# Transposes of x1 in every fourth product step, and the last rows of x1 loaded two at a time, in an encoder block on one core

## The chip, the cores and the metric

The kernel runs as one program on one core of a Trainium2 chip. The metric is the device time of that program in microseconds (us). Before the change three runs gave 2173.34, 2176.47 and 2177.3 us, so the median is 2176.47 us.

## What is computed

One layer works on 2048 tokens of 1024 channels in float32. A mixer (input projection, a pooling branch, a convolution branch, gates, output projection) gives x1, and an MLP follows. Only its end matters here:

```python
x = x + rmsnorm(merged @ w_o[l], norm_mix_post[l])        # this sum is x1
h = rmsnorm(x, norm_mlp_pre[l])
f = jnp.square(jax.nn.relu(h @ w_up[l])) @ w_down[l]
x = x + rmsnorm(f, norm_mlp_post[l])
```

Here `w_up` is 1024 x 4096 and `w_down` is 4096 x 1024. The last line needs every row of x1 once more, after the last product.

## The kernel before, in words

**Numbers and halves.** Every operand of a product is held as a high part `hi` and a low part `lo`, and a product of two tiles is three matmul passes (hi-hi, hi-lo, lo-hi). The 2048 tokens are two halves `b` of 1024, and each half is two blocks `t` of 512. Products are done in Strassen's manner, with seven products `i` = 1 to 7 where eight plain ones would stand.

**The down stage.** The product with `w_down` is the last stage. It runs over four slabs `s` (rows of `w_down`), and `jobs` lists its steps: for slabs 0 to 2 the seven products of `DOWN`, each for both halves, and then slab 3 (`LAST`), first all seven products of `DOWN_LAST` = 1, 6, 7, 4, 2, 5, 3 for half 0 and then all seven for half 1. One product of slab 0 was already done earlier as filler, so 55 products stand in the list. `down_product` does a product as two steps `h` = 0, 1 of 24 matmuls each (`token_product`, matmuls on L1708), and adds each step's result to an accumulator in SBUF on VectorE (L120). So the stage has 110 product steps and 2640 matmuls.

**What a product needs.** `token_cells` loads a product's tokens (`tr<-fd`) into buffers of the pool TR (9 buffers of 128 x 1024), casts them to `hi` on ScalarE (L1688) and subtracts on VectorE to get `lo` (L123). `weights_down` loads the weights (`wr<-w_down`, in slab 3 also `wr<-wsum`), casts them on ScalarE (L1647 in slab 3) and gets their low part either on VectorE (`wl`, L123) or, in slab 3, by a load (`wl<-lows`). The low parts have three buffers (pool `pwl`), so the load of one waits until TensorE has finished with the weights three loads earlier. All these loads are issued by SyncE (`load`, L129), which takes its list in order: an entry that waits for a buffer holds up all that stand behind it.

**Background work.** After each product step `bg()` calls every `Lane`. A lane holds generators and a rate. At each call it takes up to `rate` pieces from its generator; a piece that yields a number n makes the lane skip the next n - 1 calls. Instructions of a lane are only ordered behind the main line's last instruction when the program's lists are made; on the chip they run when their engine's list comes to them.

**The transposes.** x1 lies in DRAM with channels on partitions (`x1d`). `turned` (L1770) makes a copy with tokens in rows (`x1t`) in 16 pieces: two loads of 256 KB into a TR buffer `x`, issued by GpSimd (`aside`, L133), `yield 2`, one transpose on VectorE into a second TR buffer `y` (L1784), four stores of 128 KB from `y`, again by GpSimd, and `yield`. Its lane has rate 2 and starts with the second product of the stage.

**The end.** For each half and block an object `Finish` waits until its accumulators are complete, takes squares on ScalarE (L1811) and multiplies by the gain on VectorE (`gain`, L126), computes the inverse root (`root`), loads rows of x1t in four pieces of 512 KB (`fetch`, `big<-x1t`, SyncE) into the pool BIG, adds the scaled result to them (`cell`, L1831) and stores them (`put`: GpSimd for half 0, SyncE for half 1). The blocks of half 0 do this in a lane during the products of half 1. The last block, (1, 1), uses `last_steps` for its loads and first gains; its end is `at_end`, called from inside the last product (`leave`, L1881, which also stores on SyncE). `last_steps` fetches all four pieces in the first call after it was made, that is, at the first product step of half 1.

Of the kernel before, what the change touches and what calls it, by code (L numbers as in the profile page):

```python
# [18 lines left out]
T = 512  # L19
G = T // P  # L20
# [47 lines left out]
def block_kernel(  # L68
# [15 lines left out]
    nc = tc.nc  # L84
# [17 lines left out]
    def nm(s):  # L102
        seq[0] += 1
        return f"{s}_{seq[0]}"

    def mk(pl, tag, dt=F32, shape=(P, TB)):
        return pl.tile(list(shape), dt, tag=tag, name=nm(tag))
# [4 lines left out]
    def two(ap):  # L112

        return ap.rearrange("p (c t) -> p c t", c=2)
# [4 lines left out]
    def add(o, a, b):  # L119
        return nc.vector.tensor_tensor(o, a, b, op=ALU.add)  # L120
# [4 lines left out]
    def mul(o, a, b):  # L125
        return nc.vector.tensor_tensor(o, a, b, op=ALU.mult)  # L126

    def load(o, src):
        return nc.sync.dma_start(o, src)  # L129

    def aside(o, src):

        return nc.gpsimd.dma_start(o, src)  # L133
# [8 lines left out]
    def mark(i):  # L142
        marks[i.ins.engine] = i.ins
        return i
# [119 lines left out]
    def psum(lab):  # L264
        return ps_mm.tile([P, TB], F32, tag="mm", name=nm(lab))
# [197 lines left out]
    def root_psum():  # L463
        return mk(ps_rb, "rb", F32, (P, T))
# [138 lines left out]
    def tr(dt=F32):  # L603
        return mk(*TR, dt)

    whole = tr()[:, :P]
# [927 lines left out]
    n = [0]  # L1534
# [29 lines left out]
    LAST = SLABS - 1  # L1564
    DOWN = (5, 6, 1, 3, 7, 4, 2)
    DOWN_LAST = (1, 6, 7, 4, 2, 5, 3)
    ENDS = {(0, 0): 2, (1, 0): 4, (1, 1): 5, (0, 1): 3}
    wsum, lows = {}, {}

    def last_weights():  # L1570
# [122 lines left out]
    chains, tiles = {}, {}  # L1693

    def banks(ps):
        return [ps[:, :T], ps[:, T:]]
# [41 lines left out]
    def recombine(b, pairs):  # L1738

        for to, of in pairs:  # L1740
            for o in (0, 1):
                add(acc[to, o, b], acc[to, o, b], acc[of, o, b])
                yield

    def last_product(i, h, b, w, cells):

        if i in (1, 2, 5):
            if i == 5 and b:
                chains[i, h] = [root_psum() if h else psum("down")[:, :T] for _ in (0, 1)]
            else:  # L1750
                tiles[i, h] = psum("down")
                chains[i, h] = banks(tiles[i, h])
        of = {1: 1, 6: 1, 7: 1, 4: 1, 2: 2, 5: 5, 3: 5}[i]
        ps, whole = chains[of, h], tiles.get((of, h))
        final = (i, b) == (DOWN_LAST[-1], 1)
        m, t = {1: (0, 0), 6: (0, 1), 7: (1, 1), 4: (1, 0), 2: (0, 0), 5: (1, 1), 3: (0, 1)}[i]
        c = acc[{(0, 0): 2, (0, 1): 3, (1, 0): 4, (1, 1): 5}[m, t], h, b]
        then = fin[b, t].at_end(h, c, ps) if final else None
        token_product(ps, w, cells, h, start=i in (1, 2, 5), stop=i in (4, 2, 3), after=then)
        if final:  # L1760
            return
        if i == 5 and b:
            for q, half in zip(ps, banks(c)):
                mark(add(half, half, q))
        else:
            mark(add(c, c, whole))
        if i == ENDS[m, t]:
            fin[b, t].ready[m, h] = c

    def turned():  # L1770
        for b in range(NB):
            for t in (0, 1):
                to = x1t[b, t].rearrange("(n tb i) (q k j) -> n q i tb k j", n=2, i=32, q=4, j=32)
                for c in (0, 2):
                    for n in (0, 1):
                        x, y = mk(*TR), mk(*TR)
                        s = slice(n * (T // 2), (n + 1) * (T // 2))
                        for k in (0, 1):
                            aside(
                                x[:, k * T : (k + 1) * T].rearrange("p (k n) -> p k n", k=2),  # L1780
                                two(x1d[b, c + k, t])[:, :, s],
                            )
                        yield 2
                        nc.vector.transpose(  # L1784
                            y.rearrange("p (tb k j) -> p k tb j", k=4, j=32),
                            x.rearrange("p (k tb j) -> p k tb j", k=4, j=32),
                        )
                        for q in range(4):
                            aside(
                                to[n, q][:, :, 2 * c : 2 * c + 4],  # L1790
                                y[32 * q : 32 * q + 32].rearrange("p (tb k j) -> p tb k j", k=4, j=32),
                            )
                        yield
# [4 lines left out]
    class Finish:  # L1798
# [36 lines left out]
            return [self.ready[m, g // 2][:, s] for m in (0, 1)]  # L1835

        def put(self, g):
            (load if self.b else aside)(out[self.b, self.t, g], self.x[g])

        def steps(self, lag):  # L1840
            for k in ((0, 0), (0, 1), (1, 0), (1, 1)) if self.t == 0 else ((1, 0), (1, 1), (0, 0), (0, 1)):
                while k not in self.ready:
                    yield 1
                self.gain(*k)
                yield
            for g in range(2):
                self.fetch(g)
            r = self.root(0, G)
            yield lag
            for g in range(G):  # L1850
                if g + 2 < G:
                    self.fetch(g + 2)
                self.cell(g, r[:, g : g + 1], self.parts(g))
                self.put(g)
                yield

        def last_steps(self):
            for g in range(G):
                self.fetch(g)
            for k in ((1, 0), (1, 1)):  # L1860
                while k not in self.ready:
                    yield 1
                self.gain(*k)
                yield

        def at_end(self, h, c, ps):
            y = tr()
            halves = [slice(i * T, (i + 1) * T) for i in (0, 1)]

            def arrive(gg):  # L1870
                s = halves[gg]
                mark(add(c[:, s], c[:, s], ps[gg]))
                self.squares(0, h, c[:, s], gg)
                mul(y[:, s], c[:, s], gains[0][:, :T])

            def leave(g, r):
                to = out[self.b, self.t, g]
                part = [y[:, halves[g % 2]], self.ready[1, h][:, halves[g % 2]]]
                x = self.x[g]
                for m, s in list(enumerate(halves))[::-1]:  # L1880
                    nc.vector.scalar_tensor_tensor(x[:, s], part[m], r, x[:, s], op0=ALU.mult, op1=ALU.add)  # L1881
                    load(to[:, s], x[:, s])

            def after(gg):
                with tc.high_priority(offset=URGENT):
                    arrive(gg)
                    if gg:
                        r = self.root(2 * h, 2 * h + 2)
                        for g in (0, 1):
                            leave(2 * h + g, r[:, g : g + 1])  # L1890

            return after

# [46 lines left out]
    for n, (s, i, b) in enumerate(jobs):  # L1940
        if s < LAST and i == DOWN[0] and b == 0:
            part = weights_down(s)
        if s == LAST and i == DOWN_LAST[0]:
            part = weights_down(s)
            if b == 0:
                gains.append(mk(p_ws, "ws"))
                load(gains[0], post)
                junk.append(mk(p_ws, "ws"))
                lanes += [Lane(3, fin[0, 0].steps(3), fin[0, 1].steps(3))]
            else:  # L1950
                lanes += [Lane(2, fin[1, 0].steps(1)), Lane(2, fin[1, 1].last_steps())]
        if s == LAST or b == 0 or (s, i) in [(0, i) for i in FIRST]:
            w = [part(i, o) for o in (0, 1)]
        if s == 0 and b and i in FIRST:
            for o in (0, 1):
                acc[i, o, 0] = mk(*BIG)
                load(acc[i, o, 0], fill[i, o])
        if n == 1:
            lanes.append(Lane(2, turned()))
        cells = coming.pop(0)  # L1960
        while len(coming) < (2 if s == LAST else 1) and n + 1 + len(coming) < len(jobs):
            job = jobs[n + 1 + len(coming)]
            coming.append(token_cells(*job, BIG if n < 4 else TR))
        down_product(s, i, b, w, cells)
        if s == LAST - 1 and i == 1:
            lanes.append(Lane(1, recombine(b, ((2, 1), (1, 6), (7, 1), (1, 5), (3, 1)))))
        if s == LAST - 1 and i == 7:
            lanes.append(Lane(1, recombine(b, ((4, 7), (5, 7)))))
        if (s, i, b) == (LAST - 1, DOWN[-1], 1):
            empty()  # L1970
# [71 lines left out]
```

## Time and profile before

| | |
|---|---|
| median of three runs | 2176.47 us |
| the profiled execution's own time | 2174.86 us |
| its span, first to last instruction | 2173.1 us |
| around the span | 1.76 us |
| TensorE matmuls busy | 2135.3 us, 98% |
| VectorE busy | 1716.1 us, 79% |
| ScalarE busy | 1034.3 us, 48% |
| mean DMA rate | 266 GB/s |
| mean granted clock of TensorE | 0.995 |

Times in the trace count from the span's start. The down stage fills the part from 1539 us on. In a row of the timeline stand the start, the length, the engine, the line, the operation with its tiles, a count, and in brackets the idle time ahead of it and what ended it. A row of waits has the total, the number of times and the longest. SPq is SyncE's list of DMA issues, and `DMA tr<-x1d` is the time from a DMA's issue to its landing. A matmul is shown with its whole passage (0.39 us), but one starts every 0.227 us when nothing holds it up.

### The profile page before, as it was taken

To read this page: it belongs to the slowest core of one execution; us is meant where nothing else is said; L and a number is where in the kernel's file an instruction comes from. 1 tells how busy PE (TensorE), PEld (TensorE's weight loads), DVE (VectorE), ACT (ScalarE), POOL (GpSimd) and SP (SyncE) were. 2 spreads that over 40 slices of the span, in tenths; PEclk is the share of its full clock that TensorE was granted. 3 is DMA by queue.
4 is the path that set the end of the run, shared out by engine and by line. 5 is a ranking of instruction groups with operands and counts; after the bars stand their busy time and mean duration, and the time that the engine had idled before them with its cause. 6 is when DMAs were issued, how large, how long until landed. Compare 5 with 4: busy or idle time off the path is not lost.

```text
span 2173.1 us, 25018 instructions
## 1 busy us (share of the span) xinstructions
PE 2135.3 (98%) x9424; PEld 1759.1 (81%) x9424; DVE 1716.1 (79%) x1664; ACT 1034.3 (48%) x1119; POOL 74.8 (3%) x131
## 2 busy tenths in 40 slices
PE   9999999999999999999999999999999999999996
PEld 7778888888888888888888888888887788888875
DVE  8999788999789999997777857876655775687557
ACT  6444453334534655445635766665443332223442
POOL 0000000000000000000000000000122300000000
PEclk9999999999999999999999999999999999999998
DMA  4789998688897787336686768986987775445896
GB/s 177 267 301 330 342 353 311 228 286 305 320 342 271 262 303 268 136 116 233 249 335 227 267 249 307 360 284 240 345 277 280 257 257 173 163 145 187 298 365 235
DMA packets 167498, 578.54 MB, mean 266 GB/s; under 512 B 20304, under 2 KB 24528, under 8 KB 167376
## 3 DMA queue, kind: packets, MB, share of 16 engines
q1 hardware_dynamic: 145616, 501.42, 64.4%
q10 hardware_dynamic: 12672, 46.14, 5.5%
q0 software_dynamic: 9088, 29.37, 3.9%
q8 instruction: 74, 1.21, 0.2%
q14 instruction: 48, 0.39, 0.1%
HBM read 381.20 MB, written 195.65 MB: 265 GB/s over the span
## 4 chain that ended last, share of the span: by engine, by line
PE 73%; DVE 9%; DMA 9%; issue 5%; ACT 2%; POOL 1%; SPq 0%; DVEq 0%; ACTq 0%; POOLq 0%
PE up L252 28%; PE down L1708 18%; PE wo L252 7%; PE glu L252 5%; PE B L252 4%; PE ga L252 3%; PE gb L252 3%; DVE y L910 3%; PE pool L252 2%; DMA tr<-x1d 2%; PE A L252 2%; DMA wl<-lows 1%; DMA tr<-fd 1%; POOL x1t L133 1%; DVE wl L123 1%
## 5 line engine op out<-in xcount | busy, mean ns | idle before, releaser
L252 PE MATMUL up<-big,wh 128*128 128x512 f32 x1792 | 480.9, 390 | 1.2 <-DVE big L123 0.8
L252 PEld LDWEIGHTS up<-big,wh 128*128 128x128 f32 x1792 | 335.8, 188 | 71.9 <-DVE big L123 1.1
L209 ACT CAST wh<-wr 128x1024 fp32r<-128x1024 f32 x167 | 175.5, 1052 | 314.9 <-PE up L252 68.5
L1708 PE MATMUL down<-wh,tr 128*128 128x512 f32 x784 | 307.0, 392 | 3.2 <-DVE tr L123 3.2
L910 DVE SCALAR_TENSOR_TENSOR y<-v,cst,y 128x1024 f32<-128x1024 f32 x240 | 307.0, 1279 | 2.4
L1708 PE MATMUL down<-wh,fo 128*128 128x512 f32 x776 | 298.6, 390 | 0.5 <-ACT wh L209 0.5
L252 PE MATMUL up<-big,wl 128*128 128x512 f32 x896 | 275.9, 389 | 0.0
L1708 PE MATMUL down<-wl,fo 128*128 128x512 f32 x760 | 235.1, 391 | 3.0 <-DVE wl L123 3.0
L209 ACT CAST wh<-ws 128x1024 fp32r<-128x1024 f32 x124 | 130.5, 1053 | 220.1 <-PE up L252 74.7
L252 PEld LDWEIGHTS up<-big,wl 128*128 128x128 f32 x896 | 168.2, 188 | 35.1
L1688 ACT CAST fo<-tr 128x1024 fp32r<-128x1024 f32 x86 | 90.4, 1051 | 219.2 <-DMA tr<-fd 90.8
L123 DVE TENSOR_TENSOR wl<-ws,wh 128x1024 fp32r<-128x1024 f32 x116 | 141.4, 1219 | 46.8 <-ACT wh L209 46.3
L1708 PEld LDWEIGHTS down<-wh,tr 128*128 128x128 f32 x784 | 148.0, 189 | 35.2 <-DVE tr L123 4.3
L1708 PEld LDWEIGHTS down<-wh,fo 128*128 128x128 f32 x776 | 145.9, 188 | 31.4 <-ACT wh L209 0.9
L1708 PEld LDWEIGHTS down<-wl,fo 128*128 128x128 f32 x760 | 142.7, 188 | 34.6 <-DVE wl L123 5.3
L123 DVE TENSOR_TENSOR wl<-wr,wh 128x1024 fp32r<-128x1024 f32 x111 | 135.1, 1218 | 26.0 <-ACT wh L209 22.9
L120 DVE TENSOR_TENSOR big<-big,down 128x1024 f32<-128x1024 f32 (+1 forms) x84 | 99.8, 1189 | 70.4 <-PE down L1708 70.3
L123 DVE TENSOR_TENSOR tr<-tr,fo 128x1024 fp32r<-128x1024 f32 x86 | 104.7, 1219 | 46.2 <-ACT fo L1688 46.0
L252 PE MATMUL glu<-big,wh 128*128 128x512 f32 x432 | 117.5, 393 | 3.0 <-ACT tr L408 2.5
L252 PE MATMUL wo<-big,wh 128*128 128x512 f32 x448 | 120.2, 390 | 0.0
L252 PE MATMUL gb<-big,wh 128*128 128x512 f32 x448 | 120.1, 390 | 0.0
L252 PE MATMUL ga<-big,wh 128*128 128x512 f32 x448 | 119.8, 389 | 0.0
(208 smaller groups left out, 3383.0 us busy)
## 6 DMA issues: line engine op xcount, KB each, us to landing
tr<-fd SPq DMA_DIRECT2D x110, 512.0 KB, 4.5
wr<-w_down SPq DMA_DIRECT2D x68, 512.0 KB, 6.3
wl<-kept SPq DMA_DIRECT2D x67, 512.0 KB, 5.2
kept<-wl SPq DMA_DIRECT2D x66, 512.0 KB, 5.7
wr<-w_up SPq DMA_DIRECT2D x64, 512.0 KB, 4.5
wr<-w_in SPq DMA_DIRECT2D x56, 512.0 KB, 6.0
fd<-tr ACTq DMA_DIRECT2D x54, 512.0 KB, 3.5
fd<-tr SPq DMA_DIRECT2D x48, 512.0 KB, 3.3
```

The lines of the kernel that those rows point to most:

```text
L120: return nc.vector.tensor_tensor(o, a, b, op=ALU.add)
L123: return nc.vector.tensor_tensor(o, a, b, op=ALU.subtract)
L133: return nc.gpsimd.dma_start(o, src)
L209: nc.scalar.copy(hi[:, :n], src[:, :n])
L252: i = nc.tensor.matmul(ps, w[wp][:, (at + k) * P : (at + k + 1) * P], rhs[k][xp], start=start and n == 0, stop=stop and n == len(order) - ...
L910: nc.vector.scalar_tensor_tensor(acc, v[:, k : k + TB], wk, acc, op0=ALU.mult, op1=ALU.add)
L1688: nc.scalar.copy(hi, t)
L1708: i = nc.tensor.matmul(ps[gg], cells[j][xp][:, c * T + at : c * T + at + P], w[j][wp][:, c * T : (c + 1) * T], start=start and first, stop ...
```

## The change

It does two things. In `turned` the number behind the loads goes from 2 to 4, so that a lane of rate 2 does a piece of the transposing in every fourth product step. In `last_steps` the four loads no longer stand ahead of everything: block (1, 1) first waits for its accumulator (1, 0), takes its gain, and then asks for rows 0 and, at the next piece, 1; then the same for (1, 1) and rows 2 and 3. Those two accumulators are complete after the two steps of product 5 of half 1, the last but one product.

The other lines of the diff give the same values, the same queue and the same order as before for every job in the list: `ENDS` comes out with the same numbers, the keys of `chains` and `tiles` get a third part, `put` names the queues that `load` and `aside` stand for, no `lag` is zero, and `after` takes the same roots and rows.

```diff
@@ last_product
-            if i == 5 and b:
-                chains[i, h] = [root_psum() if h else psum("down")[:, :T] for _ in (0, 1)]
+            tiles.pop((i, h, b), None)
+            if (i == 5 and b and h == 0) or (b and h and i == 5):
+                chains[i, h, b] = [root_psum() if h else psum("down")[:, :T] for _ in (0, 1)]
@@ turned
-                        yield 2
+                        yield 4
                         nc.vector.transpose(
@@ put
-            (load if self.b else aside)(out[self.b, self.t, g], self.x[g])
+            (nc.gpsimd if self.b == 0 else nc.sync).dma_start(
+                out[self.b, self.t, g], self.x[g]
+            )
@@ steps
-            yield lag
+            if lag:
+                yield lag
@@ last_steps
-            for g in range(G):
-                self.fetch(g)
-            for k in ((1, 0), (1, 1)):
+            for n, k in enumerate(((1, 0), (1, 1))):
                 while k not in self.ready:
                     yield 1
                 self.gain(*k)
                 yield
+                self.fetch(2 * n)
+                yield
+                self.fetch(2 * n + 1)
+                yield
```

More of the change, by code (lines that the diff above doesn't have):

```diff
@@ L1566, in block_kernel @@
     DOWN_LAST = (1, 6, 7, 4, 2, 5, 3)
-    ENDS = {(0, 0): 2, (1, 0): 4, (1, 1): 5, (0, 1): 3}
+    ENDS = {(0, 0): max((1, 2), key=DOWN_LAST.index), (1, 0): 4, (0, 1): 3, (1, 1): max((5, 7), key=DOWN_LAST.index)}
     wsum, lows = {}, {}
@@ L1747, in last_product @@
         if i in (1, 2, 5):
-            if i == 5 and b:
-                chains[i, h] = [root_psum() if h else psum("down")[:, :T] for _ in (0, 1)]
-            else:
-                tiles[i, h] = psum("down")
-                chains[i, h] = banks(tiles[i, h])
+            tiles.pop((i, h, b), None)
+            if (i == 5 and b and h == 0) or (b and h and i == 5):
+                chains[i, h, b] = [root_psum() if h else psum("down")[:, :T] for _ in (0, 1)]
+            else:
+                tiles[i, h, b] = psum("down")
+                chains[i, h, b] = banks(tiles[i, h, b])
         of = {1: 1, 6: 1, 7: 1, 4: 1, 2: 2, 5: 5, 3: 5}[i]
-        ps, whole = chains[of, h], tiles.get((of, h))
+        ps, whole = chains[of, h, b], tiles.get((of, h, b))
         final = (i, b) == (DOWN_LAST[-1], 1)
@@ L1761, in last_product @@
             return
-        if i == 5 and b:
+        if whole is None:
             for q, half in zip(ps, banks(c)):
@@ L1886, in after @@
                     arrive(gg)
-                    if gg:
-                        r = self.root(2 * h, 2 * h + 2)
+                    if h:
+                        if gg:
+                            r = self.root(2, 4)
+                            for g in (2, 3):
+                                leave(g, r[:, g - 2 : g - 1])
+                    elif gg:
+                        r = self.root(0, 2)
                         for g in (0, 1):
-                            leave(2 * h + g, r[:, g : g + 1])
+                            leave(g, r[:, g : g + 1])
             return after
@@ L1944, in block_kernel @@
             part = weights_down(s)
+        if s == LAST and i == DOWN_LAST[0]:
             if b == 0:
```

## The prediction

> **What bounds the kernel now.** I read the page first: the busy times of the engines.
>
> ```profile
> PE 2135.3 (98%) x9424; PEld 1759.1 (81%) x9424; DVE 1716.1 (79%) x1664; ACT 1034.3 (48%) x1119; POOL 74.8 (3%) x131
> ```
>
> TensorE is busy for 98% of the span, so a change that touches no matmul can only win what TensorE loses by standing still, or what it loses by a slower clock. Both parts of this change lie in the down stage, so I looked next at that stage in the chain of waits, and at TensorE's last matmuls in the timeline.
>
> ```profile
> 1539.37 27.21 PE down L1708 x120
> ...
> 1760.03 298.62 PE down L1708 x1316
> ...
> 2115.76 12.44 DMA wl<-lows
> ```
>
> ```profile
> 2159.61 0.61 PE L1708 MATMUL rb<-wl,big 128*128 128x512 f32 x2
> ```
>
> The first of these rows gives the pace: 27.21 / 120 = 0.2268 us from one matmul to the next. The code has 55 products of 48 matmuls in the stage, 2640 in all, which would take 2640 x 0.2268 = 598.7 us. The stage takes from 1539.4 to about 2160.2, 620.8 us. So it loses 22.1 us, and that is the most that both parts together can bring. From 1760.03 on there is one unbroken piece of 298.62 us for 1316 matmuls (0.2269 each): nothing is lost there. The losses lie ahead of 1760, while the transposes run, and behind 2058, in the last slab. The view of who waited for whom, for TensorE, names them:
>
> ```profile
> PE down L1708 <- DMA wl<-lows: 8.0, 3, 6.2
> PE down L1708 <- DVE tr L123: 3.2, 2, 1.8
> PE down L1708 <- DVE wl L123: 3.0, 4, 1.3
> PE down L1708 <- ACT wh L209: 0.5, 1, 0.5
> ```
>
> Asked by stretches, the same view puts the last three rows between 1640 and 1760, and the first, the loads of low parts, behind 2058. They add up to 14.7 us of pure waiting; the other 7.4 us of the 22.1 are matmuls at a slower pace after a wait.
>
> **First part: the transposes.** Work is only moved: 16 transposes, 32 loads and 64 stores stay. First the row of the change itself, VectorE's timeline around one transpose, and TensorE's at the same time:
>
> ```profile
> 1651.27 1.25 DVE L1784 STREAM_TRANSPOSE tr<-tr 128x1024 f32<-128x1024 f32 x1 [3.32 <-DMA tr<-x1d]
> 1652.44 1.18 DVE L123 TENSOR_TENSOR tr<-tr,fo 128x1024 fp32r<-128x1024 f32 x1
> ```
>
> ```profile
> 1653.68 0.50 PE L1708 MATMUL down<-wh,tr 128*128 128x512 f32 x1 [1.80 <-DVE tr L123]
> ```
>
> VectorE stood for 3.32 us in front of the transpose because its piece of x1d had not landed. The next entry of VectorE's list makes the low part of a token tile, and TensorE waited 1.80 us for exactly that. The chain of waits shows why the load is late:
>
> ```profile
> 1660.43 3.12 DMA tr<-x1d
> ...
> 1663.62 1.26 DVE tr L1784
> ```
>
> From one transpose (1651.27) to the next (1663.62) a closed loop runs: transpose, four stores issued by GpSimd, two loads issued behind them, landing, transpose. It took 12.35 us. The lane asks for a transpose every second product step, that is every 48 x 0.2268 = 10.9 us. The loop is longer than its period, so VectorE waits in front of transposes again and again. The view of the tensor x1d gives the total, with the number of times:
>
> ```profile
>   DVE tr L1784: 29.6, 8
> ```
>
> With a transpose in every fourth step the period is 21.8 us, 9.4 us more than the loop. The 29.6 us of VectorE's waiting should vanish nearly whole. The second thing that late pieces do is to keep TR buffers. SyncE's own waits, from 1540 to 1760 and then from 1760 to 1910, are led by:
>
> ```profile
> SPq L129 <- DMA x1t<-tr: 60.4, 14, 8.5
> ```
>
> ```profile
> SPq L129 <- PE down L1708: 97.6, 28, 7.8
> ```
>
> While transposes run, SyncE's loads of tokens wait for buffers that the stores of x1t have not given back; without them SyncE only waits for TensorE, which is the healthy case. At half the rate each buffer `y` still waits for its stores, but there is twice as long between two of them. The buffer `x` on the other hand is now taken for 64 product steps, about 350 us, where it was taken for 32.
>
> The price: of the 22.1 us, the last slab has 9.1 (below) and about 2 around the two small waits for low parts (8.0 - 6.2 = 1.8 us, with a little slow pace). The rest, 22.1 - 9.1 - 2 = 11 us, belongs to the transposes. Bounds: all 11 us are won, or none, if the shortage of buffers and not the wait for x1d carries it, or a loss, if the shortage lasts twice as long (a rival below). I take 8 us, near the upper end, because the quoted wait of TensorE follows directly on a wait for x1d, and leave 3 for waits by buffers. What is added at 1760 to 1900 is 16 / 2 = 8 transposes of 1.25 us on VectorE, hidden by the unbroken TensorE piece in that stretch; if that cover is gone they cost at most 10 us.
>
> **Second part: the last rows.** TensorE's timeline around the longest wait:
>
> ```profile
> 2121.69 0.39 PE L1708 MATMUL down<-wh,tr 128*128 128x512 f32 x1
> 2128.25 1.22 PE L1708 MATMUL down<-wl,big 128*128 128x512 f32 x2 [6.17 <-DMA wl<-lows]
> ...
> 2135.57 0.40 PE L1708 MATMUL down<-wh,fo 128*128 128x512 f32 x1
> ```
>
> By the code 20 matmuls lie between the first start of this fence plus one pace (2121.92) and the last row. At pace they take 4.54 us and would end at 2126.46; they end at 2135.57. So the wait of 6.2 us costs 9.1 us, 2.9 of them because the first matmuls behind it run at about half speed (1.22 us where a pair has 0.61). [...] The trace has the duration, so 9.1 is used.
>
> The load that came late was issued at 2115.76 and took 12.44 us. What SyncE issued ahead of it:
>
> ```profile
> 2097.32 1.37 SPq L129 DMA_DIRECT2D big<-x1t  x3
> ...
> 2107.71 0.43 SPq L129 DMA_DIRECT2D big<-x1t  x1
> 2108.24 0.87 SPq L129 DMA_DIRECT2D wr<-wsum  x2
> 2109.16 1.40 SPq L129 DMA_DIRECT2D big<-x1t  x2
> 2110.66 1.19 SPq L129 DMA_DIRECT2D wr<-wsum  x2
> 2113.07 1.54 SPq L129 DMA_DIRECT2D big<-x1t  x2
> ```
>
> Eight pieces of x1t go out in 16 us. Four belong to block (0, 1), which is due then; by the order of the lanes the first four are those of `last_steps`, not needed before 2162. What the DMA engines can move shows in the row of the stretch from 2050 to 2100:
>
> ```profile
> 2050.00:2100.00 50.00, 48.15 (x212) 39.22 (x211) 33.40 (x46) 25.06 (x43) 2.14 (x4) 1.00 0.94 350
> ```
>
> They are full (0.94) at 350 GB/s, so a piece of 512 KB takes 1.5 us, and four pieces 6.0 us. Without them the late load lands at about 2128.2 - 6.0 = 2122.2. TensorE wants it at 2121.92. So the wait of 6.2 us shrinks to some 0.3 us, too short for the clock, and 8.6 us of the 9.1 are won. Bounds: none, if the load is late for its other neighbours; 9.1, if it is on time. I take 8.
>
> What is late next: VectorE's additions, which give PSUM tiles back.
>
> ```profile
> 2119.12 2.74 DVE L1831 SCALAR_TENSOR_TENSOR big<-big,sy,big 128x512 f32<-128x512 f32 x4 [7.83 <-DMA big<-x1t]
> ...
> 2127.83 1.21 DVE L120 TENSOR_TENSOR big<-big,down 128x1024 f32<-128x1024 f32 x1
> ```
>
> Block (0, 1) waits 7.83 us for its own rows of x1t, and the addition behind it ends at 2129.0. Product 5 begins half a product behind 2135.57, at 2138.3; with the wait for low parts gone it would ask for that tile 9.1 us sooner, near 2129.2. This just fits, and as these rows too now have four pieces less ahead of them, it should fit easily.
>
> The moved loads: rows 0 and 1 go out during product 5, rows 2 and 3 during product 3. SyncE has these entries there now, and VectorE wants the rows at:
>
> ```profile
> 2151.52 18.34 SPq L129 DMA_DIRECT2D out<-big  x12
> ```
>
> ```profile
> 2162.54 2.74 DVE big L1881 x4
> ...
> 2166.76 0.75 DVE big L1881
> ```
>
> ```profile
> DMA to landing us min/median/max: 4.4/9.3/12.4
> ```
>
> Rows 2 and 3 are asked for behind the first step of product 3 (2138.3 + 10.9 + 5.4 = 2154.6), ahead of most of the stores, and land at the median (9.3) at 2163.9, 2.9 us before their use. I charge nothing for them. Work and bytes are the same in both kernels.
>
> **The sum.** 8 and 8 us are 16 us. On the profiled execution's own time this is 2174.9 - 16 = 2158.9; that execution is 1.6 us under the median of the runs, so the time to expect is 2160.5, rounded to 2160. The other edits give the same values and cost nothing.
>
> **The rivals.** (a) Only one part works. Either the shortage of TR buffers carries the loss ahead of 1760 and stays, or the low parts stay late for 2 to 6 us because of block (0, 1)'s rows, or the loads of `last_steps` are put early in SyncE's list all the same, since they are only ordered behind the main line. Each leaves one gain of about 8: 2168. For it speaks the 60.4 us of SyncE's waiting; against it that the two stalls are in different places with different causes.
>
> (b) The rows come late. [...] As a mechanism here: the list of SyncE puts rows 2 and 3 behind the stores of rows 0 and 1, which wait for the first four L1881 (end 2165.3). Then they land 4.4 to 12.4 us later, at 2169.7 to 2177.7, where 2166.76 is wanted: 3 to 11 us at the end that nothing hides, 2163 to 2171. Against it: VectorE's work ahead of that is long, so the loads should be ready first when the list is made.
>
> (c) Slower: `x` holds one of nine TR buffers for twice as long, and SyncE's shortage lasts for twice as many products. If the 60.4 us of waiting become 120.8 and TensorE pays the same share as now (11 / 60.4 = 18%), the first part loses 11 us more and the second wins 8: 2179. It is slower than before by over 0.2% from a share of (11 + 8 + 4.4) / 120.8 = 19% on; at 25%, 30 us, it gives 2176.5 + 19 - 8 = 2187. For it: after 1760 there is no slack in TR that the trace would show. Against it: these waits are 14 for 16 transposes, so they seem to go with the transposes, whose number stays, and not with the products.
>
> **The numbers.** My forecast has 0.58, (a) 0.16, (b) 0.09, (c) 0.17. A difference of 0.2%, 4.4 us, is about what a measurement of this kernel can tell from none. Faster by more: all of the forecast, 0.13 of (a), 0.07 of (b), together 0.78. Within it: 0.03 of (a), 0.02 of (b), 0.08 of (c), together 0.13. Slower: 0.09, from (c). The range goes from 2152, where the 22.1 us are won whole on the profiled execution, to 2174, past (a) and (b); outside are most of (c) and a little beneath.
>
> **What would show it.** Right: in the new profile VectorE waits for x1d no more than a few us in total, transposes run to about 1900, no TensorE wait of over 1 us lies ahead of 1900, the low part of product 2 in half 1 lands within 7 us, and four loads of x1t stand behind 2130. Wrong: SyncE's waits for x1t's stores grow beyond 60 us with TensorE waits for `tr` or `wl` behind 1760; or L1881 waits for x1t at the end; or the wait for `lows` in the last slab stays at some us.

## The result, and the profile after

The changed kernel took 2157.2 us (median of four runs, 2155.84 to 2159.0) and the kernel before 2176.76 us (four runs, 2173.34 to 2177.3). The ratio is 0.9914 with a 95% interval of 0.9897 to 0.9931: faster by 0.86%, or 19.6 us by the medians, where 16 were forecast. The two profiled executions differ by 2174.86 - 2156.01 = 18.85 us. One execution of the changed kernel in a later call, the profiled one there, was granted a mean clock of 0.39 and took 5387 us, and one of the kernel before 0.774 and 2599 us; no median, ratio or trace below counts them.

The head of the page after, and the long pieces of the down stage in its chain of waits (start, length, what):

```profile
PE 2128.9 (99%) x9424; PEld 1756.7 (82%) x9424; DVE 1716.3 (80%) x1664; ACT 1034.6 (48%) x1119; POOL 74.8 (3%) x131
```

```profile
1539.61 530.99 PE down L1708 x2340
2070.62 6.64 DMA wl<-lows
2077.31 7.56 PE down L1708 x32
2086.78 9.52 DMA big<-x1t
...
2100.14 23.43 PE down L1708 x101
```

```profile
2140.62 0.61 PE L1708 MATMUL rb<-wl,big 128*128 128x512 f32 x2
```

Where there was a patchwork of transposes, GpSimd issues and loads between 1570 and 1760, one piece of 2340 matmuls now stands, at 530.99 / 2340 = 0.2269 us each. The stage takes from 1539.5 to 2141.2, 601.8 us. By the working of the prediction it lost 22 us before; now it loses 601.8 - 598.7 = 3 us. What TensorE waits for in the stage:

```profile
PE down L1708 <- DVE tr L123: 1.5, 1, 1.5
...
PE down L1708 <- DMA wl<-lows: 0.4, 1, 0.4
```

Both waits lie in the last slab. The transposes, in the view of x1d (the issues of its loads with first and last start, and who waited for them):

```profile
L133 POOL DMA_DIRECT2D tr<-x1d x32: 713/723/736, 1535.9 to 1873.6; - x32
...
  DVE tr L1785: 2.9, 1
```

The last of these loads goes out at 1874 where it went out at 1736, the last transpose starts at 1905 where it started at 1748, and VectorE waits once for 2.9 us, not eight times for 29.6. SyncE's own waits from 1540 to 1760 are led by others than x1t's stores:

```profile
SPq L129 <- DVE wl L123: 62.2, 7, 16.0
SPq L129 <- DVE ws L123: 46.9, 6, 15.1
```

SyncE's list ahead of the load that had come late, and at the end:

```profile
2096.14 0.42 SPq L129 DMA_DIRECT2D big<-x1t  x1
2096.65 0.86 SPq L129 DMA_DIRECT2D wr<-wsum  x2
2097.56 0.93 SPq L129 DMA_DIRECT2D big<-x1t  x2
2105.71 14.12 SPq L129 DMA_DIRECT2D wl<-lows  x4
...
2139.22 0.38 SPq L129 DMA_DIRECT2D big<-x1t  x1
2141.59 0.34 SPq L1839 DMA_DIRECT2D out<-big  x1
2141.98 0.43 SPq L129 DMA_DIRECT2D big<-x1t  x1
```

```profile
2147.77 0.75 DVE big L1887
```

The load of low parts that had come late is now issued at 2105.71. In the 18.5 us ahead of it three pieces of x1t go out where eight did, and the last two pieces are issued at 2139.2 and 2142.0, between stores of block (1, 0). VectorE takes row 2 at 2147.77 with no wait. It starts on row 3 at 2149.2.

### The profile page after: what moved, and what is told of

It reads as the page before. It is cut to its first block, busy times and chain, and to the rows that moved or that the text cites. A ratio compares the mean times of both kernels' runs of the same rounds, so it can differ in the third digit from the quotient of the medians.

```text
span 2154.2 us, 25028 instructions
## 1 busy us (share of the span) xinstructions
PE 2128.9 (99%) x9424; PEld 1756.7 (82%) x9424; DVE 1716.3 (80%) x1664; ACT 1034.6 (48%) x1119; POOL 74.8 (3%) x131
## 4 chain that ended last, share of the span: by engine, by line
PE 85%; DVE 8%; DMA 3%; issue 2%; ACT 1%; SPq 0%; DVEq 0%; ACTq 0%
PE up L252 28%; PE down L1708 26%; PE wo L252 7%; PE glu L252 5%; PE B L252 4%; PE gb L252 4%; PE A L252 4%; PE ga L252 4%; PE pool L252 3%; DVE y L910 3%; DMA kept<-ws 1%; DVE tr L120 1%; DVE wl L123 1%; PE rb L458 1%; DVE ws L123 0%
## 5 line engine op out<-in xcount | busy, mean ns | idle before, releaser
L120 DVE TENSOR_TENSOR big<-big,down 128x1024 f32<-128x1024 f32 (+1 forms) x84 | 100.2, 1193 | 74.1 <-PE down L1708 74.0
```

## The experiments

Eleven kernels ran beside the changed one, each the changed kernel with one edit. The table has the median, the ratio to the kernel before on the same chip with its interval, and from the profiled execution what the down stage lost: its length less 598.7 us, and, summed from the gaps between matmuls and rounded, what of it lies in its first 400 us and behind. The split is good to about 1 us. The kernels were timed in several calls and on more than one chip, so the ratio compares better than the median.

| kernel | median us | ratio | lost | first 400 us | behind |
|---|---|---|---|---|---|
| before | 2176.8 | 1 | 22 | 10 | 12 |
| changed | 2157.2 | 0.9914 [0.9897, 0.9931] | 3 | 0 | 3 |
| yield 4 alone | 2161.7 | 0.9935 [0.9910, 0.9959] | 9 | 0 | 9 |
| late rows alone | 2173.0 | 0.9982 [0.9968, 0.9996] | 19 | 14 | 5 |
| yield 3 | 2171.7 | 0.9974 [0.9961, 0.9987] | 17 | 14 | 3 |
| yield 2, loads first | 2161.9 | 0.9932 [0.9906, 0.9958] | 9 | 5 | 4 |
| rows 0, 1 early | 2161.6 | 0.9932 [0.9906, 0.9958] | 6 | 0 | 6 |
| yield 1 | 2222.0 | 1.0207 [1.0179, 1.0235] | 65 | 60 | 5 |
| one TR buffer less | 2159.9 | 0.9917 [0.9899, 0.9935] | 4 | 0 | 4 |
| yield 2 from product 20 | 2165.2 | 0.9945 [0.9928, 0.9963] | 12 | 1 | 11 |
| yield 3 from product 2 | 2171.7 | 0.9991 [0.9977, 1.0005] | 19 | 16 | 3 |
| yield 4 from product 2 | 2160.3 | 0.9936 [0.9918, 0.9953] | 6 | 1 | 5 |
| yield 5 | 2170.9 | 0.9982 [0.9968, 0.9995] | 16 | 11 | 5 |

The changed kernel was also timed a second time, beside the last three kernels of the table:

> The changed kernel itself once more, beside these three on the same chip, to see how far one execution differs from another: 2157 us within 2, TensorE loses 3 to 5 us in the down stage.

Its median was 2158.5 us, the ratio 0.9935 [0.9911, 0.9959] where the first timing gave 0.9914. The executions of one kernel in one call lie up to 13 us apart (the kernel before: 2170.72 to 2183.37), so a few us between two medians of four executions are nothing to explain. What was expected of its stage has no trace to check it.

The other edits of the diff have no run of their own, but the traces of the first two runs below bear on them. With yield 2 every engine works through the same order of operations and tiles as in the kernel before up to 2097 us, and with the old `last_steps` the same order from 1978 us on, where those edits lie. So there are two parts to try.

**Each part alone.** `last_steps` as before with yield 4, and yield 2 with the new `last_steps`:

```diff
# yield 4 alone: last_steps as before        # late rows alone
-            for n, k in enumerate(...):     -                        yield 4
+            for g in range(G):              +                        yield 2
+                self.fetch(g)
+            for k in ((1, 0), (1, 1)):
...
-                self.fetch(2 * n)
...
-                self.fetch(2 * n + 1)
...
```

> The first part alone: yield 4, the last rows asked for early as before. My theory (the two losses are separate, each part removes its own): 11 us less than the kernel before, about 2166 us; no TensorE wait ahead of 1900 us; the wait for lows in product 2 of half 1 stays, 5 to 7 us. Rival (the gain comes from one part, and the other rode along): either 2157 us, or 2176 us.

> The second part alone: yield 2, the last rows late. My theory: 8 us less than the kernel before, about 2168 us; the waits for tr and wl between 1640 and 1760 us stay at some 6 us, the wait for lows falls under 1 us. Rival (the gain comes from one part): 2157 or 2176 us.

Measured: 2161.7 and 2173.0 us. The traces bear out that each part removes its own loss: the pace 10 to 14 us in the first 400 us, the rows 6 us behind (9 to 3 with yield 4, 12 to 5 with yield 2). In the times the pace alone is worth 14 us by the medians and 9 to 20 by the interval, where 11 were expected. The rows alone are worth 3 us by the medians and 1 to 7 by the interval, where 8 were expected. And yield 4 alone has the ratio of the changed kernel's second timing, 0.9935. So what the rows add to the pace is read from single traces; the times do not resolve it. TensorE's waits in the last stretch with yield 4 alone:

```profile
PE down L1708 <- DMA wl<-lows: 6.4, 3, 5.6
```

**How much a piece of x1t costs.** Rows 0 and 1 asked for early, rows 2 and 3 late:

```diff
+            for g in range(2):
+                self.fetch(g)
             for n, k in enumerate(((1, 0), (1, 1))):
...
-                self.fetch(2 * n)
-                yield
-                self.fetch(2 * n + 1)
-                yield
+                if n:
+                    self.fetch(2)
+                    yield
+                    self.fetch(3)
+                    yield
```

> The changed kernel, but rows 0 and 1 of the last block are asked for early, as before the change, and rows 2 and 3 late. My theory (each early piece of 512 KB takes the DMA engines about 1.5 us ahead of the low part's load): TensorE waits 2 to 4 us for lows in product 2 of half 1, and with the clock the time is 2159 to 2161 us. Rival (a threshold: the wait comes with four pieces or not at all): no wait over 1 us and 2157 us, or the whole 6 us and 2162 us.

TensorE's waits from 1960 on, and the time to landing of the loads of low parts from 1950 on: this kernel, then the landing with all four early (yield 4 alone), and with none (the changed kernel).

```profile
PE down L1708 <- DMA wl<-lows: 3.6, 3, 2.8
```

```profile
DMA to landing us min/median/max: 3.4/4.6/9.1
```

```profile
DMA to landing us min/median/max: 3.4/4.7/11.6
```

```profile
DMA to landing us min/median/max: 3.4/4.7/6.6
```

The two upper maxima, 9.1 and 11.6 us, are those of the load that TensorE waits for, at product 2 of half 1. In the changed kernel this load, issued at 2105.71, landed after 6.2 us; the 6.6 us belong to another load. In all three runs it is issued some 6 us ahead of its use, so TensorE's wait for it is what it takes beyond that: nothing, 2.8 and 5.6 us with none, two and four pieces asked for early. The landing grows by 2.9 us for the first two pieces and by 2.5 for the next two, 1.35 us for each. That is nearly a straight line and no threshold, so the rival falls. The time, 2161.6 us with runs from 2157.7 to 2166.1, cannot resolve it; the trace does.

**Is the closed loop the cause ahead of 1760?** A slower pace that is still longer than the loop, and the old pace with the loop opened, the next piece's loads issued ahead of the transpose:

```diff
# yield 3                                    # yield 2, loads first (the core)
-                        yield 4             +            x = coming
+                        yield 3             +            coming = piece(*keys[at + 1])
...                                          ...
                                                          nc.vector.transpose(
...
                                             +            yield 2
```

> The changed kernel with yield 3 in place of 4: a transpose every 16.3 us. Loop theory (the loop of transpose, stores, loads, landing takes 12.35 us and only has to be shorter than the period): as good as the changed kernel, 2157 us within 2, TensorE waits ahead of 1900 us under 1 us in all. Buffer theory (the share of TR buffers that the pieces take sets the loss, and it falls with the pace): about half of the 11 us comes back, 2162 us.

> The changed kernel at the old pace, a transpose in every second step, but the loads of the next piece are issued ahead of the transpose and the stores of this one, which takes a third TR buffer at times. Loop theory: the loop is open, VectorE waits less than 5 us in all for x1d, and the time is that of the changed kernel, 2157 to 2160 us. Buffer theory: more buffers taken at the old pace, so the loss stays or grows, 2168 us or more.

With the loads first VectorE never waits for x1d, and the loss in the first 400 us falls to 5 us from 10 to 14: the loop is a cause, and its opening is worth about half or more (the edit also moves other entries of the lists). SyncE waits as long for the stores of x1t as before (67.8 us against 60.4), so these waits do not carry the part that is gone. But with yield 3 VectorE's wait is also small (7.5 us), and 14 us are lost all the same. The theory that the loop only has to be shorter than the period fell here as a full account. So I made the pace faster than the loop allows, took a buffer away at the new pace, and put the old pace elsewhere.

```diff
# yield 1          # one TR buffer less                        # yield 2 from product 20
-  yield 4         +        held = mk(*TR)                     -  yield 4
+  yield 1         +        nc.gpsimd.memset(held[:, :1], 0.0) +  yield 2
                   ...                                         -        if n == 1:
                   +        nc.gpsimd.memset(held[:, :1], 1.0) +        if n == 20:
```

> The changed kernel with yield 1: a transpose asked for in every product step, 5.4 us, less than half the loop. Loop theory: the transposes cannot go faster than now, VectorE waits over 60 us in all for x1d, and the loss ahead of 1760 us is over 14 us: 2171 us or more. List theory (what counts is where the lists of SyncE and VectorE put token and weight loads, not the wait for x1d itself): the loss does not follow the wait; anything from 2157 to 2171 us, with TensorE waits behind loads of fd or weights.

> The changed kernel with one TR buffer held by an unused tile from the first to the last transpose, so that eight are left. Buffer theory: with one buffer less at the new pace 3 to 11 us come back, 2160 to 2168 us, and SyncE waits for x1t's stores again. Loop theory: no change, 2157 us within 2.

> The changed kernel at the old pace, a transpose in every second step, but begun at product 20 of the stage in place of product 1. Loop theory: the same loop is too long for the same period, VectorE waits some 30 us for x1d and TensorE loses 8 to 14 us as in the run of the second part alone: 2166 to 2173 us. Rival (the loss needs the first 20 products, in which token tiles are still sums of two loads and VectorE has more to do per product): VectorE waits as long, but TensorE loses under 4 us: 2157 to 2161 us.

With yield 1 VectorE's waits for x1d come to 41.1 us, short of the 60 expected, but TensorE loses 65 us, 60 of them in the first 400 us. Its waits up to 1760:

```profile
PE down L1708 <- ACT fo L1688: 35.8, 6, 11.9
PE down L1708 <- DVE tr L123: 10.7, 6, 4.9
```

Token tiles come late. In the kernel before that was one half of the waits (3.2 us for `tr`, beside 3.0 for `wl`); here it is nearly all, and many times larger. One TR buffer less at the new pace changes nothing that can be told (2159.9 us, loss 4 where it was 3): the new pace does not hang on the ninth buffer. The run from product 20 says the same from the other side. SyncE's first row of waits, from 1760 to 1960:

```profile
SPq L129 <- DMA x1t<-tr: 88.4, 20, 10.0
```

It waits longer for the buffers of x1t's stores than the kernel before (60.4 us), and TensorE does not stand once in that stretch. VectorE, too, does not wait for x1d, so my expectation of 30 us of waiting was wrong. GpSimd's list shows why. First the kernel before, then this run:

```profile
1647.22 0.73 POOL L133 DMA_DIRECT2D tr<-x1d  x1 [1.16 <-DVE tr L123]
1652.93 1.75 POOL L133 DMA_DIRECT2D x1t<-tr  x3 [4.97 <-DVE tr L1784]
1658.86 0.58 POOL L133 DMA_DIRECT2D x1t<-tr  x1 [4.18 <-issue]
1660.43 1.43 POOL L133 DMA_DIRECT2D tr<-x1d  x2 [0.98 <-issue]
```

```profile
1813.67 1.44 POOL L133 DMA_DIRECT2D tr<-x1d  x2 [1.23 <-issue]
1816.89 1.17 POOL L133 DMA_DIRECT2D x1t<-tr  x2 [1.78 <-DVE tr L1785]
1819.10 0.58 POOL L133 DMA_DIRECT2D x1t<-tr  x1 [1.04 <-issue]
1822.24 0.59 POOL L133 DMA_DIRECT2D x1t<-tr  x1 [2.56 <-issue]
1823.17 1.43 POOL L133 DMA_DIRECT2D tr<-x1d  x2 [0.34 <-issue]
```

In the kernel before one of the next piece's two loads (1647.22) stands ahead of the four stores and the other (the first of the two at 1660.43) behind them, and the transpose at 1663.62 starts when that one has landed. In this run both loads of the next piece (1813.67) stand ahead of the stores, as in the run with the loads first. The loop is open here, although the lane is the same: from the third piece on the loads land 5.6 to 11.5 us before their transpose, and the transposes lie 11.0 us apart on average, close to the 10.9 asked for. The kernel before has a load behind the stores up to its twelfth piece and none from the thirteenth on (its transpose starts at 1712.55), and all its waits for x1d lie ahead of 1690. So VectorE waits where GpSimd's list closes the loop, and not wherever the pace is two steps. Why the list comes out closed early in the stage and open later is not shown. What the late start loses instead, 11 us, lies behind: TensorE waits twice for an addition of VectorE (3.2 us in all, L120), once for a token tile (1.9 us) and twice for the last slab's low parts (1.2 us), and behind the two longest of these waits (2.5 and 1.9 us) about eight matmuls start some 0.43 us apart, where 0.23 is usual. Why the additions come late is not shown either.

**What does yield 3 lose?** I counted in SyncE's list, for each token load, the weight loads of later products that stand ahead of it. With yield 3 from product 1 this is ten for the seventh and eighth pieces of token tiles, with yield 4 six. Three kernels asked whether this count or the pace decides.

```diff
# yield 3 from product 2         # yield 4 from product 2         # yield 5
-                yield 4         -        if n == 1:              -                yield 4
+                yield 3         +        if n == 2:              +                yield 5
-        if n == 1:
+        if n == 2:
```

> Yield 3 again, but the transposes begin one product later. In SyncE's list of the run with yield 3 from product 1, ten weight loads of later products stand ahead of the token loads for the seventh and eighth pieces of token tiles in the stage, where the changed kernel has six; here six or seven stand there. List theory (TensorE loses where too many weight loads, which wait for buffers, stand ahead of token loads): loss ahead of 1900 us under 4 us, 2157 to 2161 us. Pace theory (a transpose every 16.3 us is too often): the loss of 15 us stays, 2168 to 2172 us.

> The changed kernel, but the transposes begin one product later. At most nine weight loads stand ahead of any early token load. List theory and pace theory alike: no loss ahead of 1900 us over 2 us, 2155 to 2160 us.

> Yield 5, a transpose every 27 us, more than twice the loop. Ten weight loads stand ahead of the seventh to ninth pieces of token tiles in SyncE's list, as in the run with yield 3. List theory: TensorE waits for tokens around 1650 us though VectorE hardly waits for x1d, a loss of 5 to 15 us, 2162 to 2171 us. Pace theory: no loss, 2157 us within 2.

Yield 5 is the clearest case: the slowest pace of all, VectorE does not wait for x1d, and the stage loses 16 us, 11 of them early. The pace theory falls. SyncE's list and TensorE's wait at that place:

```profile
1621.92 22.64 SPq L129 DMA_DIRECT2D wr<-w_down  x7
1644.65 7.88 SPq L129 DMA_DIRECT2D tr<-fd  x8
```

```profile
1655.65 0.79 PE L1708 MATMUL down<-wh,fo 128*128 128x512 f32 x1 [3.02 <-ACT fo L1688]
```

For 22.6 us SyncE works through seven weight loads, waiting for their buffers, and eight token loads stand behind them. They go out one behind the other from 1644.65 on, land 7.3 to 10.0 us after their issue, and TensorE stands. This is what the list theory expected, at the place it named; with the slower matmuls behind the wait, 0.43 us apart, it makes some 7 of the 11 us. Yield 4 from product 2 lost 1 us in the first 400 us, so it was as good as yield 4 there, as both theories had it. But yield 3 from product 2 lost 16 us where my count foresaw under 4. Its first row of SyncE's waits, from 1540 to 1760:

```profile
SPq L129 <- DVE wl L123: 74.1, 6, 24.2
```

Again SyncE stands up to 24.2 us in front of weight loads with token loads behind, so the mechanism is there; the count of loads is a bad measure of it. The three runs with 3 or 5 lose 11 to 16 us early, and the runs with 4 lose 1 us or none. An odd number puts pieces by turns behind the first and the second step of a product. Whether that is what spoils the lists stays open.

## Why the prediction was right, point by point

**The time, the side and the range** were right: 2157.2 us against 2160, within 2152 to 2174.

**The bound.** That only TensorE's 22 us of lost time could be won, 11 ahead of 1760 and 11 in the last slab, was right in the main: the trace has 10 and 12, 19 of the 22 came, and no other stage moved by more than executions differ among each other.

**The first part** was put at 8 us of 11, with 3 left for buffers. In the changed kernel's trace the loss is gone whole, 10 us. The step "VectorE waits for x1d, and TensorE waits right behind" held: the wait went from 29.6 to 2.9 us, and opening the loop at the old pace brought about half of the gain or more. The loop itself was read too simply. It is closed only where GpSimd's list puts a load behind the stores, and the 12.35 us are one turn of it: from the third to the twelfth piece the transposes of the kernel before lie 8.6 to 15.3 us apart. The step "a period of 21.8 us is longer than the loop, so the loss vanishes" was incomplete: periods of 16.3 and 27 us are longer too, and lose 11 to 16 us. At 21.8 us SyncE's list also happens to serve the token loads in time. I did not name this list as a condition, and it was luck that the number 4 meets it. The 3 us left for the shortage of TR buffers were not needed, and the experiments show no loss from it.

**The second part** was put at 8 us. The mechanism was right, down to the transfer: four pieces of x1t ahead of the low part's load made it late. The size was off: 6 us in the traces, and in the times at yield 4 too little to tell from none. (Product 5 begins half a step, 12 matmuls, behind the fence's last row, not half a product; the time given for it, 2138.3, is right.) A piece delays by 1.35 us, not by 1.5: the prediction took the 350 GB/s of 2050 to 2100, and in the trace of the kernel before the DMA engines moved 380 GB/s from 2100 to 2120, which gives 1.38 us for 512 KB. And 3 us of other losses stay in the last slab, among them 1.5 us in a wait for tokens that the prediction did not have. So the first part brought 2 us more than its 8 and the second 2 us less, and these two errors cancel. That the last slab also lost 2 to 3 us less with the pace alone (12 to 9) stood in no term; the sum of 16 was about 3 us short of the 19 in the traces, and still well inside the range.

**The clock.** In the kernel before the granted clock was 0.50 from 2128 to 2132, behind the 6.2 us wait. That halved pace is gone with the wait, as the term of 2.9 us had it: the short waits of the changed kernel, 0.4 and 1.5 us, are followed by matmuls at the usual distance but for the first, and the granted clock was 1.00 behind both. That some 0.3 us would be too short to slow the matmuls agrees with this wait of 0.4 us, and with waits of 0.7 and 1.1 us in the last slab of the kernel before, behind which the same holds. But a wait much shorter than 6.2 us can halve the pace too. Behind the wait of 2.8 us in the run with two early pieces eight matmuls start 0.43 us apart, where 0.23 is usual. Nine runs have a wait of 1.8 to 2.0 us for a token tile in the last slab; in five of them seven or eight matmuls behind it start about 0.43 us apart, in four none do. So a wait of 2 us costs 1.5 us more in some executions and nothing more in others.

**The moved loads.** Rows 2 and 3 go out at 2139.2 and 2142.0, between the stores of block (1, 0), and no L1887 waits. They are issued 8.6 and 7.2 us before their use and land 2.9 and 1.9 us before it, so the charge of nothing was right. They go out 4 to 6 us later in the last product than the prediction had them, and take 5.6 and 5.3 us to land where it took 9.3; these two errors cancel. To issue them early would have kept the loads where they were, and the traces speak against it here: issued late, they cost nothing at their use, and the load of low parts that TensorE needs sooner landed after 6.2 us, where it took 11.6 with all four early.

**The rivals.** (a) was wrong in both halves by the traces: both parts work, and apart; the times show the first part alone clearly and the second alone barely. (b) did not come. (c), the doubled shortage of TR buffers, is refuted by the changed kernel itself, where SyncE's waits for the stores of x1t are gone from 1540 to 1760, and by the run with one buffer less; in the run from product 20 these waits are longer and TensorE does not stand. A slower outcome did exist nearby, but for another reason: yield 1, at which VectorE waits 41.1 us for x1d and token tiles come late.

## What to carry to other kernels

A load that is issued early is not free when a more urgent one comes behind it, which here landed 1.35 us later for each 512 KB ahead of it: count the bytes ahead of each load that has little time, and move the others behind it. A background step that goes through DMAs of its own can close a loop, here one of 12.35 us: look in the issuing engine's list whether its next loads stand ahead of its stores, and put them there. A period longer than the loop is not enough by itself, as 3 and 5 steps show, which lost 11 to 16 us early. And a change of pace rearranges every list that is made at build time, so try the neighbouring values: here 3, 4 and 5 gave 2171.7, 2157.2 and 2170.9 us.

## What was not expected of the hardware

One and the same load of 512 KB took 6.2, 9.1 or 11.6 us to land with no, two or four unneeded loads of the same size ahead, 1.35 us for each, in a stretch where the DMA engines were full, with a busy share of 1.02 from 2104 to 2112 in the changed kernel and of 1.00 from 2115.8 to 2128.2 in the kernel before. The best load of its kind took 3.4 us. And SyncE's list, which is worked through in order, passed a wait on in one burst: in the run with yield 5 eight token loads behind 22.6 us of waiting weight loads took 7.3 to 10.0 us to land, where the median of this kernel's token loads in the stage is 6.1 us. A short wait of TensorE can cost more than its length: after a wait of 1.8 to 2.0 us, seven or eight matmuls started about 0.43 us apart, where 0.23 is usual, in five of nine traces.
